# Moving the context's state and the first running sum to later levels inside the GLA heads of a hybrid backbone block

## Chip, cores and metric

The kernel runs on one core of one Trainium2 chip. The metric is the device time of one execution in microseconds (us). The engines are named as in the profile: PE is TensorE (matmul), PEld its weight loads, DVE VectorE, ACT ScalarE, POOL GpSimd, SP SyncE.

## What is computed

One backbone layer on 512 latent tokens and 256 context tokens of width 2048. One projection feeds four heads of gated linear attention (GLA, here *gated heads*) and four mLSTM heads, both run in two directions; an output projection, and a convolutional SwiGLU MLP follow. The gated heads, which the change concerns, compute this:

```python
def gla_scan(k, v, log_a, s0, q=None):      # chunked over CHUNK positions
    def step(s, inp):
        bcum = jnp.cumsum(ac, axis=2)
        b_end = bcum[:, :, -1, :]
        k_to_end = kc * jnp.exp(b_end[:, :, None, :] - bcum)
        s_new = jnp.exp(b_end)[..., None] * s + jnp.einsum('bhik,bhiv->bhkv', k_to_end, vc)
        ...
        scores = jnp.einsum('bhjk,bhik,bhjik->bhji', qc, kc, jnp.exp(rel))
        o = (jnp.einsum('bhji,bhiv->bhjv', scores, vc)
             + jnp.einsum('bhjk,bhkv->bhjv', qc * jnp.exp(bcum), s))
```

The context runs through this scan without queries; its last state is the state in which each latent scan begins. `log_a`, the decay, is a log-sigmoid of a low-rank projection.

## The kernel before

**Stages.** The program goes through modulation and the projections of heads 0 and 1 (to about 200 us), then a woven part (200 to 480 us), the mLSTM heads (to about 1060 us), the MLP (1076 to 2420 us) and a tail. The change lies in the woven part. There gated head *h* is worked on while PE also computes the projection of a later head: heads 0 and 1 beside the projection of head 2, head 2 beside that of head 3, head 3 and the gates of the mLSTM heads (`ml_gates`) beside that of head 4.

**Weaving.** `weave(stages, steps)` interleaves two generators. A stage yields how much PE time is wanted as cover, and `weave` takes steps of the projection until that debt is paid; what is overpaid stays as credit. A step is one *group* `a_0` to `a_5` of one pair of 128-row weight tiles (`kp`, 8 of them): a_0 and a_1 are six matmuls of 512 columns, a_2 and a_3 twelve of 256, a_4 and a_5 six of 384. They count as 1.36, 1.36, 1.44, 1.44, 1.04 and 1.04. The pair `fill` is what a gated head yields: `fill[0]` behind each level of scores, `fill[1]` behind each part between: (1.75, 0.85) in heads 0 and 1, (4.1, 2) in head 2, (2.7, 1.3) in head 3. In this part PE's instructions keep the program's order (`tc.keep_in_program_order`). The order on DVE, ACT and SP is chosen by a scheduler. All engines run their queue in order.

**One gated head** (`gla`). `sd` is the diagonal of the scores. Then seven levels of scores follow, 0 to 6: `ex` (decays; two DVE subtractions, two exponentials, a DVE product with q and k), matmuls `sl` (L801 to L804), and a DVE copy under a mask of `sl` into `sc` (L805). Between them stand:

- behind level 0, in head 0 only, `next(first, 1)` (L810): it makes the context's running sum `csum` on PE out of `cla`, and from it `kd`, the context's decay, by an exponential. `first` is `gla_prep(0)`, whose earlier steps made `cdec` (PE) and `cla` (DVE, L672). The other heads have all steps of `gla_prep` done by the head before: `after`, one step behind each of levels 2 to 6 (`dec` twice, PE, each with the `la` product on DVE L672; `cdec`, with `cla`; `csum`; the scans).
- behind level 1, the context's state `cst`: products of `kd` with the keys on DVE, eight matmuls on PE, a copy into `s0` on ACT (L818 to L825). Then `qi` and `kt` (decayed queries and keys for the latent states; ACT exponentials, DVE products).
- behind levels 2 and 3, `ktt`: a transposition of `kt` on PE and a copy on ACT (L846).
- behind levels 4 to 6, `st`: the latent states, matmuls on PE and two DVE products each (L856). The first of them reads `s0`.

At the end come the four outputs `po` (order 1, 2, 0, 3), for each a square on ACT (L869) and a copy to `ob` on DVE (L870), and later the transpositions `yt`.

**Banks.** The six groups of the projection hold six of the eight PSUM banks. All other PE results of the woven part (`sd`, `sl`, `dec`, `cdec`, `csum`, `cst`, `ktt`, `st`, `po`, `yt`, and `pre`, `pa`, `pgc` of `ml_gates`) share the other two through `psb`. So a matmul of these may start only when the reader of the bank's earlier owner is done.

**The splits.** Each `kp` needs its weights in two parts: `raw` arrives by DMA, ACT makes `hi_h` (L105), and DVE makes `lo_h` (L106), 1024 columns in one instruction.

**ml_gates** ends with two directions of the same: transpositions `pa` of `li` and `cum` (PE), `negh`, `negl` and `dg` (DVE, L928 to L932, from `pf`), and `pgc` (PE), which reads `dg`.

Of the kernel before, what the change touches and what calls it, by code (L numbers as in the profile page):

```python
# [18 lines left out]
P = 128  # L19
# [7 lines left out]
CJ = TC // P  # L27
H = 4
DK = 128
DV = 256  # L30
# [53 lines left out]
def block_kernel(ctx: ExitStack, tc: tile.TileContext, a: dict, out: bass.AP):  # L84
    nc = tc.nc
    V, S, G, PE = nc.vector, nc.scalar, nc.gpsimd, nc.tensor
# [9 lines left out]
    def mul(o, x, y):  # L96
        return V.tensor_tensor(out=o, in0=x, in1=y, op=ALU.mult).ins
# [12 lines left out]
    def mm(*args, **kw):  # L110
        ins = PE.matmul(*args, **kw)  # L111
        if pinned[0]:
            tc.keep_in_program_order(ins)

    def tr(*args):
        ins = PE.transpose(*args)
        if pinned[0]:
            tc.keep_in_program_order(ins)
# [8 lines left out]
    cst = keep.tile([P, C_END], F32, name="cst")  # L127
# [32 lines left out]
    def psb(name, shape=(P, T)):  # L160
        return banks8[0].tile(list(shape), F32, name=name, tag="acc") if banks8 else \
            psB.tile(list(shape), F32, name=name, tag="psb")

    def ytile(k, name, shape=(P, T), dtype=F32):
        return yp.tile(list(shape), dtype, name=name, tag=f"y{k}")
# [413 lines left out]
    first, early_sums = project_first()  # L579
# [40 lines left out]
    for c0, n, hs, m in ((0, T, hx, gm[0]), (T, TC, hc, gm[1])):  # L620
        ps = psb(f"gm{c0}", (P, n))
        for k in range(KT):
# [4 lines left out]
            for i, part in enumerate(parts):  # L627
                mm(ps[g : g + 32, :], wsm[:, k, :], part, start=(k < 4 and i == 0),
                   stop=(k >= 12 and i == len(parts) - 1), skip_group_check=True)
# [14 lines left out]
    def wtile(name, tag, *shape):  # L644
        return (wkh if tag in ("qk", "v", "kn", "vn") else wk).tile([P, *shape], F32, name=name, tag=tag)
# [110 lines left out]
    def level_decays(h, lv, bt):  # L756

        b = LEVELS[lv]
        n = T // (2 * b)
        ex = wk2.tile([P, 2, T], F32, name=f"ex{h}_{lv}", tag="ex")  # L760
        sf = bt[0].rearrange("p (n a b) -> p n a b", a=2, b=b)
        sb = bt[1].rearrange("p (n a b) -> p n a b", a=2, b=b)
        rf = sf[:, :, 0, b - 1 : b].unsqueeze(2).to_broadcast([P, n, 2, b])
        rb = sb[:, :, 1, 0:1].unsqueeze(2).to_broadcast([P, n, 2, b])
        sub(crossed(ex, b, True), sf[:, :, ::-1, :], rf)
        sub(crossed(ex, b, False), sb, rb)
        S.activation(ex[:, 0, :], ex[:, 0, :], AF.Exp, scale=DECAY)
        S.activation(ex[:, 1, :], ex[:, 1, :], AF.Exp, scale=-DECAY)
        return ex
# [5 lines left out]
    def gla(h, pair, qk, v, kn, vn, yT, prep, fill, after, pending, first=iter(())):  # L775
        bt, ends = prep["bt"], prep["ends"]

        sc = wtile(f"sc{h}", "sc", 2, TJ, P)
        scd = sc[:, 0]
        s0 = wtile(f"s0{h}", "state", 2, DV + 2)  # L780
        st = [s0[:, :, 0:DV], sc[:, 1].rearrange("p a b -> p (a b)").rearrange("p (d c) -> p d c", d=2)]
        mul(scd.rearrange("p a b -> p (a b)"), *qk)
        ps = psb(f"sd{h}", (P, TJ))
        for j in range(TJ):
            mm(ps[:, j : j + 1], scd[:, j, :], cst[:, C_ONE : C_ONE + 1], start=True, stop=True)
        V.scalar_tensor_tensor(out=scd, in0=ident.unsqueeze(1).to_broadcast([P, TJ, P]), scalar=2.0,
                               in1=ps.unsqueeze(2).to_broadcast([P, TJ, P]), op0=ALU.mult, op1=ALU.mult)
        yield fill[0]
        if next(first, 1) is None:
            yield fill[1]  # L790
        for lv, b in enumerate(LEVELS):
            ex = prep["ex"][lv] if lv < 2 else level_decays(h, lv, bt)
            if pair:
                done = mul(ex, ex, pair[0])
            else:
                for i in range(2):
                    done = mul(ex[:, i, :], ex[:, i, :], qk[i])
            if lv == 6:
                with tc.issue_after(done):
                    mul(qi, qi, qk[0].unsqueeze(1).to_broadcast([P, 2, T]))  # L800
            ps = psb(f"sl{h}_{lv}", (P, TJ, P))  # L801
            for i in range(TJ):
                js = slice(P * i, P * i + P)
                mm(ps[:, i, :], ex[:, 1, js], ex[:, 0, js], start=True, stop=True)  # L804
            done = V.copy_predicated(scd, msk[:, lv, :].unsqueeze(1).to_broadcast([P, TJ, P]), ps).ins  # L805
            if lv == 0:
                gate = done
            yield fill[0]
            if lv == 0:
                next(first, 1)  # L810
                for _ in pending:
                    pass
                yield fill[1]
            if lv > 1 and next(after, 1) is None:
                yield fill[1]
            if lv == 1:

                kd = prep["kd"]  # L818
                for j in range(CJ):
                    mul(kd[:, :, j], kd[:, :, j], kn[j].unsqueeze(1).to_broadcast([P, 2, DK]))  # L820
                ps = psb(f"cst{h}", (P, 2, DV))
                for d in range(2):
                    for j in range(CJ):
                        mm(ps[:, d, :], kd[:, d, j, :], vn[j][:, 0:DV], start=(j == 0), stop=(j == CJ - 1))
                S.copy(s0[:, :, 0:DV], ps)  # L825
                qi = wtile(f"qi{h}", "qi", 2, T)
                for d in range(2):
                    S.activation(qi[:, d, :], bt[d], AF.Exp, scale=DECAY)
                yield fill[1]
                kt = [ytile(10 + d, f"kt{h}{d}", (P, TJ - 1, P)) for d in range(2)]  # L830
                for d in range(2):
                    for i in range(TJ - 1):
                        S.activation(kt[d][:, i, :], bt[d][:, P * (i + d) : P * (i + d) + P], AF.Exp, scale=-DECAY,
                                     bias=ends[:, 0, d, i : i + 1])
                    x = kt[d].rearrange("p a b -> p (a b)")
                    with tc.issue_after(gate):
                        mul(x, x, qk[1][:, P * d : P * d + 3 * P])
                ktt = []
            elif lv in (2, 3):
                d = lv - 2  # L840
                ktt.append(ytile(12 + d, f"ktt{h}{d}", (P, TJ - 1, P)))
                ps = psb(f"ktt{h}{d}", (P, TJ - 1, P))
                for i in range(TJ - 1):
                    tr(ps[:, i, :], kt[d][:, i, :], ident)
                with tc.high_priority():
                    S.copy(ktt[d], ps)  # L846
                yield fill[1]
            elif lv > 3:
                n = lv - 4
                if n:  # L850
                    st.append(ytile(9 + n, f"st{h}{n}", (P, 2, DV)))
                ps = psb(f"st{h}{n}", (P, 2, DV))
                for d, i in ((0, n), (1, 2 - n)):
                    mm(ps[:, d, :], ktt[d][:, i, :], v[i + d][:, 0:DV], start=True, stop=True)
                for d, i in ((0, n), (1, 2 - n)):
                    V.scalar_tensor_tensor(out=st[n + 1][:, d, :], in0=st[n][:, d, :], scalar=ends[:, 1, d, i : i + 1],  # L856
                                           in1=ps[:, d, :], op0=ALU.mult, op1=ALU.add)
                yield fill[1]
        ssq = wtile(f"ssq{h}", "ssq", TJ)
        junk = wtile(f"junk{h}", "kn", DV)  # L860
        ob = wtile(f"ob{h}", "tmp", TJ, DV)
        for j in (1, 2, 0, 3):
            po = psb(f"po{h}_{j}", (P, DV))
            js = slice(P * j, P * j + P)
            parts = [(qi[:, d, js], st[3 - j if d else j][:, d, :]) for d in range(2)]
            parts.append((scd[:, j, :], v[j][:, 0:DV]))
            for n, (l, r) in enumerate(parts):
                mm(po, l, r, start=(n == 0), stop=(n == len(parts) - 1))
            S.activation(junk, po, AF.Square, accum_out=ssq[:, j : j + 1])  # L869
            V.tensor_copy(ob[:, j, :], po)  # L870
            yield 0.5
        return finish(h, ob, ssq, yT)
# [668 lines left out]
```

## Time and profile before

| | |
|---|---|
| time before, median of 3 runs | 2442.56 us (2441.49 to 2443.43) |
| the profiled execution's own time | 2441.44 us |
| its span in the trace | 2439.7 us |
| PE busy | 2412.9 us |
| DVE busy | 1793.3 us |
| ACT busy | 1005.2 us |
| mean granted clock of PE | 0.998 |

Times in the trace count from the start of the span. A row of the timeline has start, duration, engine, line, operation, what is written and read by the program's names without numbers, and in brackets the engine's idle time before it with what released it. Matmuls overlap: the next one starts before the modelled end of the last, so the time that a group of matmuls takes is read from its start to the next group's start. In the order of the program below, names carry numbers: `sl0_5` is the score of head 0 at level 5, `a2_1` is group 1 of the projection of head 2, `hi_h4_7` the weights of head 4 at kp 7.

### The profile page before, as it was taken

The numbers are of one execution on the slowest core, as the hardware profiler recorded it, in microseconds if no ns is written. First come the engines' busy times: TensorE is split into PE (matmuls) and PEld (weight loads), VectorE is DVE, ScalarE is ACT, GpSimd is POOL, SyncE is SP. The second block draws the span as 40 slices with busy tenths as digits, with TensorE's granted clock in tenths as the row PEclk, the third lists the DMA queues.
The fourth block names the chain that finished last, engine by engine and source line by source line (L and its number), as shares of the span: only waits on it lengthen the run. The fifth ranks groups of instructions, "written<-read, shape, count | busy, mean of one in ns | idle before, by whom it ended". The sixth has DMA issues, their size and how long they took to land.

```text
span 2439.7 us, 38673 instructions
## 1 busy us (share of the span) xinstructions
PE 2412.9 (99%) x15434; PEld 2173.7 (89%) x15434; DVE 1793.3 (74%) x2872; ACT 1005.2 (41%) x1498; POOL 175.9 (7%) x221
## 2 busy tenths in 40 slices
PE   8999999999999999999999999999999999999998
PEld 6888999899988888888898989899999999999997
DVE  6666856555456586779987887878787878787886
ACT  4225533322233232256544454445444444444445
POOL 0000000000000000000201010101011111111021
PEclk9999999999999999999999999999999999999999
DMA  9751111233455798833646464555555555546464
GB/s 388 284 173 56 46 53 44 78 121 114 137 189 191 237 321 275 287 130 109 145 132 154 116 151 123 137 134 141 136 130 139 134 143 122 146 123 154 113 185 135
DMA packets 122487, 373.67 MB, mean 153 GB/s; under 512 B 13912, under 2 KB 19010, under 8 KB 122306
## 3 DMA queue, kind: packets, MB, share of 16 engines
q1 hardware_dynamic: 95298, 318.75, 39.8%
q0 software_dynamic: 25920, 51.40, 11.7%
q8 instruction: 121, 1.98, 0.3%
q10 hardware_dynamic: 1088, 1.05, 0.1%
q14 instruction: 60, 0.49, 0.1%
HBM read 320.80 MB, written 50.34 MB: 152 GB/s over the span
## 4 chain that ended last, share of the span: by engine, by line
PE 94%; DVE 3%; DMA 1%; ACT 1%; issue 1%; SPq 0%; POOL 0%; POOLq 0%; ACTq 0%; DVEq 0%
PE a L111 19%; PE ug L111 18%; PE uv L111 18%; PE dn L111 18%; PE ga L111 7%; PE wo L111 7%; PE po L111 2%; PE ps_m L111 1%; PE sl L111 1%; PE st L111 1%; PE cst L111 1%; DMA raw_uv<-in_w_up 0%; DVE ex L94 0%; DMA xl<-in_xT 0%; DMA raw_m<-in_w_mod 0%
## 5 line engine op out<-in xcount | busy, mean ns | idle before, releaser
L111 PE MATMUL dn<-gh,lo_d 128*128 128x512 f32 x672 | 262.5, 391 | 2.3 <-DVE lo_d L106 2.3
L111 PE MATMUL dn<-gl,hi_d 128*128 128x512 f32 x672 | 261.6, 389 | 0.0
L111 PE MATMUL dn<-gh,hi_d 128*128 128x512 f32 x672 | 261.6, 389 | 0.0
L1295 DVE SCALAR_TENSOR_TENSOR cv<-pads,cwt,cv 128x512 f32<-128x512 f32 x344 | 239.2, 747 | 0.6
L1349 POOL DMA_DIRECT2D x2d<-st x160 | 140.1, 929 | 1142.0 <-ACT st L1348 1062.2
L106 DVE TENSOR_TENSOR lo_buv<-sum_uv,hi_buv 128x1024 fp32r<-128x1024 f32 x80 | 98.0, 1225 | 102.8 <-ACT hi_buv L105 102.7
L322 DVE SCALAR_TENSOR_TENSOR raw_m<-raw_m,crow 128x1024 f32<-128x1024 f32 x128 | 154.6, 1229 | 1.7 <-DMA raw_m<-in_w_mod 1.7
L111 PEld LDWEIGHTS dn<-gh,lo_d 128*128 128x128 f32 x672 | 126.1, 188 | 31.1 <-DVE lo_d L106 5.2
L111 PE MATMUL a<-hi_h,hTh 128*128 128x256 f32 x512 | 151.7, 296 | 0.5 <-ACT e L404 0.5
L111 PEld LDWEIGHTS dn<-gl,hi_d 128*128 128x128 f32 x672 | 126.2, 188 | 26.0
L111 PEld LDWEIGHTS dn<-gh,hi_d 128*128 128x128 f32 x672 | 126.2, 188 | 25.7
L111 PE MATMUL a<-lo_h,hTh 128*128 128x256 f32 x512 | 144.7, 283 | 0.0
L111 PE MATMUL a<-hi_h,hTl 128*128 128x256 f32 x512 | 144.6, 283 | 0.0
L105 ACT CAST hi_d<-raw_d 128x1024 fp32r<-128x1024 f32 x86 | 88.6, 1030 | 130.0 <-PE ug L111 70.3
L106 DVE TENSOR_TENSOR lo_d<-raw_d,hi_d 128x1024 fp32r<-128x1024 f32 x86 | 102.9, 1196 | 48.3 <-ACT hi_d L105 47.8
L111 PE MATMUL ug<-bth,hi_bug 128*128 128x256 f32 x480 | 136.8, 285 | 0.0
L111 PE MATMUL ug<-bqh,lo_aug 128*128 128x256 f32 x480 | 135.8, 283 | 0.0
L111 PE MATMUL uv<-bqh,lo_auv 128*128 128x256 f32 x480 | 135.8, 283 | 0.0
L111 PE MATMUL uv<-bth,hi_buv 128*128 128x256 f32 x480 | 135.8, 283 | 0.0
L111 PE MATMUL uv<-btl,hi_buv 128*128 128x256 f32 x480 | 135.8, 283 | 0.0
L111 PE MATMUL uv<-bth,lo_buv 128*128 128x256 f32 x480 | 135.8, 283 | 0.0
L111 PE MATMUL uv<-bql,hi_auv 128*128 128x256 f32 x480 | 135.8, 283 | 0.0
(414 smaller groups left out, 7262.7 us busy)
## 6 DMA issues: line engine op xcount, KB each, us to landing
raw_m<-in_w_mod SPq DMA_DIRECT2D x192, 512.0 KB, 5.1
raw_d<-in_w_down SPq DMA_DIRECT2D x82, 512.0 KB, 3.5
raw_ug<-in_w_up SPq DMA_DIRECT2D x80, 512.0 KB, 3.6
x2d<-st POOLq DMA_DIRECT2D x160, 256.0 KB, 5.6
raw_uv<-in_w_up SPq DMA_DIRECT2D x80, 512.0 KB, 5.4
raw_h<-in_w_heads SPq DMA_DIRECT2D x64, 512.0 KB, 3.6
raw_ga<-in_w_gates SPq DMA_DIRECT2D x32, 512.0 KB, 3.8
raw_wo<-in_w_out SPq DMA_DIRECT2D x32, 512.0 KB, 4.5
```

The lines of the kernel that those rows point to most:

```text
L105: cast[0] = S.copy(hi, x).ins
L106: return V.tensor_tensor(out=lo, in0=x, in1=hi.bitcast(F32), op=ALU.subtract).ins
L111: ins = PE.matmul(*args, **kw)
L322: V.scalar_tensor_tensor(out=x, in0=x, scalar=1.0, in1=crow[0], op0=ALU.mult, op1=ALU.mult, accum_out=mtot[:, at : at + 1])
L1295: V.scalar_tensor_tensor(out=t3, in0=src, scalar=w, in1=t3, op0=ALU.mult, op1=ALU.add)
L1349: nc.gpsimd.dma_start(x2d[k], t, accum_op=ALU.add)
```

## The change

Three things are altered in `gla`. The running sum of the first head is made behind level 1 instead of level 0. The context's state is made behind level 2 instead of level 1, in all four gated heads. And one more `yield fill[1]` stands behind it (in the old place one followed `qi`, and that one stays), so that each head asks for one more cover.

```diff
             if lv == 0:
-                next(first, 1)
                 for _ in pending:
                     pass
                 yield fill[1]
             if lv > 1 and next(after, 1) is None:
                 yield fill[1]
             if lv == 1:
-
-                kd = prep["kd"]
-                for j in range(CJ):
-                    mul(kd[:, :, j], kd[:, :, j], kn[j].unsqueeze(1).to_broadcast([P, 2, DK]))
-                ps = psb(f"cst{h}", (P, 2, DV))
-                for d in range(2):
-                    for j in range(CJ):
-                        mm(ps[:, d, :], kd[:, d, j, :], vn[j][:, 0:DV], start=(j == 0), stop=(j == CJ - 1))
-                S.copy(s0[:, :, 0:DV], ps)
+                next(first, 1)
                 qi = wtile(f"qi{h}", "qi", 2, T)
...
             elif lv in (2, 3):
+                if lv == 2:
+                    kd = prep["kd"]
+                    for j in range(CJ):
+                        mul(kd[:, :, j], kd[:, :, j], kn[j].unsqueeze(1).to_broadcast([P, 2, DK]))
+                    ps = psb(f"cst{h}", (P, 2, DV))
+                    for d in range(2):
+                        for j in range(CJ):
+                            mm(ps[:, d, :], kd[:, d, j, :], vn[j][:, 0:DV], start=(j == 0), stop=(j == CJ - 1))
+                    S.copy(s0[:, :, 0:DV], ps)
+                    yield fill[1]
                 d = lv - 2
```

Every engine issues the same instructions as before, PE 14663 matmuls and DVE 2746 instructions among them; only the order differs, from level 1 of head 0 to the end of `ml_gates`. POOL's order is the same. On SP one load (of `wlr3`) moves ahead of two weight loads of head 3. The old and the new order differ in many rows; three places follow.

The first is PE's order in head 0 at level 1, as a piece of the difference (`-` before, `+` after); `csum0` is the running sum, and the a2 rows belong to the projection of head 2.

```order
 L111 MATMUL a2_2_2070<-lo_h2_1_2178,hTh3_579 128x256
 L111 MATMUL a2_2_2070<-hi_h2_1_2177,hTl3_580 128x256
-L111 MATMUL csum0_2219<-cla0_2076,cst_58 128x128 x6
-L111 MATMUL sl0_1_2229<-ex0_1_2155 128x128 x4
+L111 MATMUL sl0_1_2220<-ex0_1_2155 128x128 x4
 L111 MATMUL a2_3_2071<-hi_h2_1_2177,hTh2_569 128x256
 L111 MATMUL a2_3_2071<-lo_h2_1_2178,hTh2_569 128x256
```

`csum0` no longer stands between the group a_2 and `sl0_1`; it comes after a_3 and a_4, where `cst0` stood, and `cst0` comes just ahead of the transposition `ktt00`.

The second is PE's order around level 5 of head 0, in two pieces of the difference: `cdec1` belongs to the preparation of head 1, `st00` to the states of head 0.

```order
 L111 MATMUL a2_0_2068<-hTl7_965,hi_h2_3_2405 128x512
 L111 MATMUL a2_0_2068<-hTh7_964,lo_h2_3_2406 128x512
-L111 MATMUL cdec1_2415<-wlr1_2306,glr_92 128x256 x2
-L111 MATMUL st00_2422<-v0_2057,ktt00_2325 128x256
-L111 MATMUL st00_2422<-v0_2057,ktt01_2373 128x256
+L111 MATMUL cdec1_2415<-wlr1_2298,glr_92 128x256 x2
 L111 MATMUL a2_1_2069<-hTh6_954,hi_h2_3_2405 128x512
 L111 MATMUL a2_1_2069<-hTl6_955,hi_h2_3_2405 128x512
```

Before, `cdec1` and `st00` stood together ahead of the group a_1; after, `cdec1` alone. The end of that group follows:

```order
 L111 MATMUL a2_1_2069<-hTl7_965,hi_h2_3_2405 128x512
 L111 MATMUL a2_1_2069<-hTh7_964,lo_h2_3_2406 128x512
+L111 MATMUL st00_2428<-v0_2057,ktt00_2325 128x256
+L111 MATMUL st00_2428<-v0_2057,ktt01_2379 128x256
 L111 MATMUL sl0_5_2439<-ex0_5_2433 128x128 x4
 L111 MATMUL a2_2_2070<-hi_h2_3_2405,hTh6_954 128x256
```

`st00` now stands right ahead of the scores `sl0_5`. In the compiled programs `sl0_5` used the bank of `st00` before and uses that of `cdec1` after; at level 5 of head 1 it is the same with `cdec2`.

The third place is the end of `ml_gates`. On PE, around `pa0` and `pgc0` in the first direction, before:

```order
 L111 MATMUL a4_1_3732<-hTl15_1785,hi_h4_7_4365 128x512
 L111 MATMUL a4_1_3732<-hTh15_1784,lo_h4_7_4366 128x512
-L116 MATMUL pa0_4382<-cst_58,li_4202 128x4 x6
-L116 MATMUL pa0_4382<-cst_58,cum_4205 128x4 x4
 L111 MATMUL a4_2_3733<-hi_h4_7_4365,hTh14_1774 128x256
 L111 MATMUL a4_2_3733<-lo_h4_7_4366,hTh14_1774 128x256
```

and at the end of the twelve matmuls of that group a_2:

```order
 L111 MATMUL a4_2_3733<-lo_h4_7_4366,hTh15_1784 128x256
 L111 MATMUL a4_2_3733<-hi_h4_7_4365,hTl15_1785 128x256
-L111 MATMUL pgc0_4413<-dg_4381,cst_58 128x16
+L116 MATMUL pa0_4394<-cst_58,li_4208 128x4 x6
+L116 MATMUL pa0_4394<-cst_58,cum_4211 128x4 x4
+L111 MATMUL pgc0_4413<-dg_4393,cst_58 128x16
 L111 MATMUL a4_3_3734<-hi_h4_7_4365,hTh14_1774 128x256
 L111 MATMUL a4_3_3734<-lo_h4_7_4366,hTh14_1774 128x256
```

Before, the group a_2 stood between `pa0` and `pgc0`; after, they are neighbours. On DVE at the same place, before:

```order
L911 SCALAR_TENSOR_TENSOR pf_4203<-li_4202 4x768 x2
L928 TENSOR_SCALAR negh_98<-pf_4203 4x512
L100 TENSOR_TENSOR cum_4205<-cum_4205,pf_4203 36x768
L929 SCALAR_TENSOR_TENSOR negl_99<-pf_4203,negh_98 4x512
L932 TENSOR_SCALAR dg_4381<-cst_58,pf_4203 4x4 x4
L928 TENSOR_SCALAR negh_98<-pf_4203 4x512
L106 TENSOR_TENSOR lo_h5_0_4492<-raw_h5_0_4489,hi_h5_0_4491 128x1024
```

and after (line numbers are higher by one behind the change):

```order
L912 SCALAR_TENSOR_TENSOR pf_4209<-li_4208 4x768 x2
L929 TENSOR_SCALAR negh_98<-pf_4209 4x512
L100 TENSOR_TENSOR cum_4211<-cum_4211,pf_4209 36x768
L106 TENSOR_TENSOR lo_h5_0_4492<-raw_h5_0_4489,hi_h5_0_4491 128x1024
L930 SCALAR_TENSOR_TENSOR negl_99<-pf_4209,negh_98 4x512
L933 TENSOR_SCALAR dg_4393<-cst_58,pf_4209 4x4 x4
L929 TENSOR_SCALAR negh_98<-pf_4209 4x512
```

The split `lo_h5_0` (for the projection of head 5) stood behind `dg` and now stands between the sum `cum` and `negl`, ahead of `dg`.

## Prediction

> **What bounds the kernel.** On the page I read first the chain of waits that ended last, as shares of the span.
>
> ```profile
> PE 94%; DVE 3%; DMA 1%; ACT 1%; issue 1%; SPq 0%; POOL 0%; POOLq 0%; ACTq 0%; DVEq 0%
> ```
>
> PE is the bound, and the change removes no PE work: it can only take away or add times in which PE stands still. So the second view is what PE waited for between 180 and 480 us (us in total, times, longest), and the third the windows of 20 us from 180 to 500, whose sum line is quoted.
>
> ```profile
> PE csum L111 <- DVE cla L672: 0.9, 1, 0.9
> PE sl L111 <- ACT ktt L846: 0.7, 1, 0.7
> PE po L111 <- DVE st L856: 0.6, 1, 0.6
> PE pa L116 <- DVE cum L100: 0.5, 1, 0.5
> PE sl L111 <- DVE sc L856: 0.4, 1, 0.4
> PE po L111 <- DVE ob L870: 0.4, 1, 0.4
> sum 320.00, PE 316.55 PEld 286.21 DVE 217.32 ACT 135.11 POOL 4.03; mean PE 19.78 PEld 17.89 DVE 13.58 ACT 8.44 POOL 0.25
> ```
>
> In these 320 us PE is idle for 320.00 − 316.55 = 3.45 us. The six stops make 3.5 of it. This is the most that the change could win in idle time, and it is 0.14% of 2442.56; 0.2% (4.9 us) is about what a measurement of this kernel can tell from no change. What the change adds has no such limit. So I followed PE's new order through the woven part, with times of the old one: at each place where the order differs, when does PE arrive, and when is what it needs ready? Times below are differences to the old run at the same work.
>
> **Head 0, level 1.** The timeline of PE and of DVE around the running sum:
>
> ```profile
> 215.44 0.72 DVE L805 COPY_PREDICATED sc<-msk,sl 128x512 f32<-128x512 uint8 x1
> 216.06 0.68 DVE L672 SCALAR_TENSOR_TENSOR cla<-cdec,ct 128x512 f32<-128x512 f32 x1
> 216.88 1.58 PE L111 MATMUL csum<-cla,cst 128*128 128x128 f32 x12 [0.88 <-DVE cla L672]
> 218.29 1.06 PE L111 MATMUL sl<-ex 128*128 128x128 f32 x8
> 219.10 0.36 PE L111 MATMUL a<-hi_h,hTh 128*128 128x256 f32 x1
> 220.62 0.34 PE L111 MATMUL a<-hi_h,hch 128*128 128x384 f32 x1
> ```
>
> `csum` waits until 216.88 for `cla`, 0.88 us. Steps from start to start: `csum` 218.29 − 216.88 = 1.41, `sl` 0.81, a group a_3 1.52. After the change `sl` of level 1 comes first. It needs the bank of level 0's `sl`, free when the mask copy ends: 215.44 + 0.72 = 216.16. PE is there at 216.88 − 0.88 = 216.00, so it waits some 0.2 us. `csum` comes after that `sl` and two groups and waits for nothing. That is −0.7. The second stop, 0.66 us behind `ktt` (`sl <- ktt`), goes too: the old `sl` of level 3 stood directly behind `ktt`, the new one has a group a_2 between. But level 2's `sl` now meets its `ex` product about as late as PE arrives; I give 0.4 back. Sum for levels 1 to 4: −1.0, bounds −1.5 (both stops, nothing back) and 0.
>
> **Head 0, level 5.** Now `sl` takes the bank of `cdec`, whose reader is `cla`:
>
> ```profile
> 238.32 0.40 PE L111 MATMUL cdec<-wlr,glr 98*128 98x256 f32 x2
> 240.88 0.69 DVE L672 SCALAR_TENSOR_TENSOR cla<-cdec,ct 128x512 f32<-128x512 f32 x1
> 240.98 0.35 PE L111 MATMUL sl<-ex 128*128 128x128 f32 x1
> ```
>
> Before, `sl` started 240.98 − 238.32 = 2.66 behind `cdec`, and `cla` ended 240.88 + 0.69 − 238.32 = 3.25 behind it. Nobody waited, as `sl` had another bank. With this bank PE waits 0.6 at the least; DVE has its two `st` products to do as well, and a_1 and `st` end later, so I take 0.95. The range is 0 (DVE does `cla` at once) to 1.5. That uses up what level 1 gave.
>
> **The outputs of head 0, the start of head 1.**
>
> ```profile
> 255.67 0.70 PE L111 MATMUL po<-st,qi 128*128 128x256 f32 x2 [0.57 <-DVE st L856]
> 259.91 0.69 DVE L97 TENSOR_TENSOR sc<-e,e 128x512 f32<-128x512 f32 x1 [0.36 <-PE po L111]
> ```
>
> `po` number 2 waited 0.57 for `st`. It now comes a group later relative to `st`'s product, so this goes, with the slow group ahead of it −0.9. But `sd` of head 1 now follows the last `po` with no group between, and its input `sc` is made by DVE only when `po` has ended (the second row: released by `po`, 0.69 long). PE waits 0.36 + 0.69 and the passing on, some 1.2, where the group a_2 hid it. Of these I count +1.0. Net +0.1, bounds −0.9 and +0.7.
>
> **Head 1.** Two new waits and one gain.
>
> ```profile
> 221.67 1.89 PE L111 MATMUL cst<-vn,kd 128*128 128x256 f32 x8
> 223.21 0.53 PE L111 MATMUL a<-hi_h,hch 128*128 128x384 f32 x1
> 275.04 0.40 PE L111 MATMUL dec<-glr,wlr 98*128 98x512 f32 x1
> 275.28 0.28 PE L111 MATMUL a<-hi_h,hTh 128*128 128x256 f32 x1
> 277.90 0.68 DVE L672 SCALAR_TENSOR_TENSOR la<-dec,lt 128x512 f32<-128x512 f32 x1
> 285.93 0.40 PE L111 MATMUL cdec<-wlr,glr 98*128 98x256 f32 x2
> 289.03 0.38 PE L111 MATMUL sl<-ex 128*128 128x128 f32 x1 [0.41 <-DVE sc L856]
> 289.50 0.68 DVE L672 SCALAR_TENSOR_TENSOR cla<-cdec,ct 128x512 f32<-128x512 f32 x1
> 303.00 0.59 PE L111 MATMUL po<-st,qi 128*128 128x256 f32 x2
> 306.15 0.48 PE L111 MATMUL po<-st,qi 128*128 128x256 f32 x1 [0.40 <-DVE ob L870]
> 307.37 0.53 PE L111 MATMUL a<-hi_h,hch 128*128 128x384 f32 x1
> ```
>
> At level 2 the order is now `dec`, a_4, `cst`, `ktt`. With two banks, `ktt` takes that of `dec`, whose reader `la` ends 277.90 + 0.68 − 275.04 = 3.54 behind `dec`. PE is there after `dec` (275.28 − 275.04 = 0.24), a_4 (221.67 − 220.62 = 1.05) and `cst` (223.21 − 221.67 = 1.54), 2.83: it waits 0.7, of which I take 0.6 (0 to 0.9). At level 5 `sl` again takes the bank of `cdec`: `cla` ended 289.50 + 0.68 − 285.93 = 4.25 behind it, `sl` itself started 3.10 behind (with a stop of 0.41). With the bank's wait that is 1.15 to 1.45 more, less if DVE's new order brings `cla` forward (0). I take 1.1. The gain is at the outputs: the last `po` took 307.37 − 306.15 = 1.22, but the two before it 306.15 − 303.00 = 3.15, 0.7 more than twice that, and the last waited 0.40 for a copy to `ob`. A group a_5 now stands between the second and the third: −1.0 (−1.3 to −0.5). Head 1: +0.7.
>
> **Heads 2 and 3.** All six stops lie outside them, since a larger `fill` puts more groups between. Head 2 loses the group between its outputs 2 and 0; four `po` in a row then wait for copies to `ob` as head 1's did. I take half of head 1's 1.0, +0.5 (0 to 1.0). Head 3: +0.1. On SP the small load of `wlr3` passes two weight loads of head 3; no stop in the waits above is one for a transfer, so this costs nothing as long as the splits, which hide it, run ahead of PE. The products with `kd` on DVE and the copy into `s0` on ACT move along with `cst`; the reader of `s0`, `st`'s product behind level 4, is still two levels away, and PE's matmuls between cover it.
>
> **The gates** hold the largest term. The wait for `pa`'s input and what follows, on PE and on DVE:
>
> ```profile
> 468.65 0.94 DVE L100 TENSOR_TENSOR cum<-cum,pf 36x768 f32<-36x768 f32 x1
> 469.52 0.67 DVE L929 SCALAR_TENSOR_TENSOR negl<-pf,negh 4x512 fp32r<-4x512 f32 x1
> 470.12 0.60 DVE L932 TENSOR_SCALAR dg<-cst,pf 4x4 f32<-4x4 f32 x4
> 471.20 1.23 DVE L106 TENSOR_TENSOR lo_h<-raw_h,hi_h 128x1024 fp32r<-128x1024 f32 x1
> 469.64 0.41 PE L116 MATMUL pa<-cst,cum 4*128 4x4 f32 x4 [0.45 <-DVE cum L100]
> 469.98 0.39 PE L111 MATMUL a<-hi_h,hTh 128*128 128x256 f32 x1
> 471.60 0.39 PE L111 MATMUL pgc<-dg,cst 4*128 4x16 f32 x2
> ```
>
> The sum `cum` starts at 468.65 and releases `pa` 0.99 later. `pa` takes 469.98 − 469.64 = 0.34, a_2 takes 1.62, and `pgc` found `dg` long done (470.72). As many groups stand between the gates' inputs `pre` and `pa` as before, so `pa` meets `cum` as before. But `pgc` now follows `pa` directly, 0.99 + 0.34 = 1.33 behind the start of `cum`, and on DVE the split of head 5 has come between: `cum` 0.87 (to the next start), the split 1.2, `negl` 0.60, `dg` 0.60, together 3.27. PE stands 3.27 − 1.33 = 1.94 before `pgc`. a_2 is not gone but moved ahead of `pa`. +2.0; without the split it would be 1.94 − 1.2 = 0.7, the lower end; the upper is 2.4, the wait of 0.45 for `cum` once more.
>
> [...]
>
> **Sum.** −1.0 + 0.95 + 0.1 + 0.7 + 0.5 + 0.1 + 2.0 = +3.35, of which I keep 3.2, as the first two places share a stop. From 480 us on the order is the same and PE is full, so nothing gives it back. The profiled execution took 2441.44 us (1.7 around its span), 1.12 below the median; a profiled run of the new kernel would take 2444.6, and the median 2442.56 + 3.2 = 2445.8. By the single bounds the sum runs from −2.5 to +7; all at one end is unlikely, so I take +1.0 to +5.2 for this case alone, of which the part over 4.9 is small.
>
> **Rivals.**
>
> *The clock closes (slower).* PE's granted clock falls when its work grows thin, as the start of the run shows (columns: window; length, busy PE, PEld, DVE, ACT, POOL; clock, DMA share, GB/s):
>
> ```profile
> 16.00:24.00 8.00, 5.16 (x56) 1.97 (x54) 5.78 (x10) 1.69 (x3) 0.00 (x0) 1.00 1.03 417
> 24.00:30.00 6.00, 4.55 (x33) 3.59 (x34) 3.18 (x9) 3.14 (x5) 0.00 (x0) 0.77 1.03 407
> 240.00:260.00 20.00, 19.43 (x116) 17.09 (x115) 18.57 (x33) 9.05 (x23) 0.00 (x0) 1.00 0.19 58
> ```
>
> After 8 us with 5.16 busy the clock was 0.77 for 6 us: 6 × 0.23 = 1.4 us lost. If the stop before `pgc` and the ones in head 1 have the same effect, two such events add 2.8: 3.2 + 2.8 = +6.0, 2448.5. It decides from stops together of some 2.8 us in 8 us, 8 − 5.16, which is more than I count in any 8 us; so 0.12. [...]
>
> *DVE falls behind and stays behind (slower).* DVE was busy 217.32 of 320 us, so it catches up in the mean; but where `cla` and `la` hold a bank, each later `sl` could wait as well. Each of the two waits in head 1 would then come twice (+1.7), and the outputs gain nothing (+1.0): +5.9, 2448.5. It decides where the mask copy behind each `sl` runs late by more than the group between. 0.12.
>
> *The change removes stops and adds none.* The five stops in heads 0 and 1: 0.88 + 0.66 + 0.57 + 0.41 + 0.40 = 2.9, which gives 2439.7. For this DVE would have to serve `cla`, `la` and `dg` ahead of the splits; the rows show the splits in front. 0.08; of it 0.03 for slow groups beside the stops vanishing as well, beyond −4.9.
>
> *Only the gates' stop fails to come,* since the split lands elsewhere in time: 3.2 − 2.0 = +1.2, 2443.8. 0.1.
>
> **Chances.** The forecast has 0.58, of which 0.07 lies over 4.9. Slower by over 0.2%: 0.07 + 0.12 + 0.12 = 0.31, less 0.02 for the second and third case falling short: 0.29. Faster: 0.03. Within 0.2%: 0.68. The predicted time is 2445.8. The range leaves out the case of no new stops and the upper end of the slow ones, from +0.4 to +6.4: 2443.0 to 2449.0. The likeliest case's own range is 2443.6 to 2447.8.
>
> **What would show it.** In the profile of the new kernel: no `csum <- cla` in the waits; `sl` of level 5 of heads 0 and 1 behind `cla`, 0.6 to 1.4 us each; `ktt` of head 1 behind `la`; `sd` of head 1 behind `sc`, about 1 us; `pgc <- dg` with about 1.9 us, the longest; PE idle of 6 to 7 us between 180 and 500 instead of 3.45. The prediction is wrong if that idle time stays under 4, if the clock of a 20 us window there falls under 0.98, or if the time changes outside 200 to 480 us.

## The result and the profile after

The changed kernel takes 2449.24 us, median of 7 runs (2448.8 to 2450.83), beside 2441.55 of the kernel before in the same series (2440.27 to 2443.43): ratio 1.0031, 95% interval 1.0022 to 1.0040. It is slower by 7.7 us. The forecast was 2445.8 with a range to 2449.0, and "within 0.2%" as the likeliest outcome. The profiled execution of the changed kernel has a span of 2447.3 us, 7.6 longer than before. The two profiles count the same instructions on both sides, 15434 matmul records on PE and 2872 on DVE (not the 14663 and 2746 named above).

The waits of PE between 180 and 490 us in the changed kernel (us in total, times, longest):

```profile
PE sl L111 <- DVE cla L672: 2.4, 2, 1.8
PE pgc L111 <- DVE dg L933: 2.0, 1, 2.0
PE sd L111 <- DVE sc L97: 0.8, 1, 0.8
PE ktt L116 <- DVE la L672: 0.6, 1, 0.6
PE pa L116 <- DVE cum L100: 0.5, 1, 0.5
PE sl L111 <- DVE ex L97: 0.4, 1, 0.4
PE sl L111 <- DVE sc L805: 0.3, 1, 0.3
PE po L111 <- DVE ob L871: 0.2, 1, 0.2
```

`csum <- cla` is gone, as it should be, and so are `sl <- ktt`, `po <- st` and the wait of `sl` for `sc` of L856. Six new waits stand in their place (`pa` is as before), all of them foreseen by name. Where the time is lost can be read from starts of the same instruction in the two traces. `sd` opens heads 1, 2 and 3, and by then both orders have done the same work; `pg` stands behind the gates. First the kernel before, then the changed one (timeline of PE):

```profile
261.14 0.95 PE L111 MATMUL sd<-cst,sc 128*128 128x1 f32 x8
312.42 0.72 PE L111 MATMUL sd<-cst,sc 128*128 128x1 f32 x6
394.41 0.83 PE L111 MATMUL sd<-cst,sc 128*128 128x1 f32 x7
482.71 0.50 PE L111 MATMUL pg<-negh,pick 4*128 4x512 f32 x2
```

```profile
261.36 0.83 PE L111 MATMUL sd<-cst,sc 128*128 128x1 f32 x6 [0.79 <-DVE sc L97]
314.12 0.95 PE L111 MATMUL sd<-cst,sc 128*128 128x1 f32 x8
396.54 0.61 PE L111 MATMUL sd<-cst,sc 128*128 128x1 f32 x5
475.61 0.36 PE L111 MATMUL pgc<-dg,cst 4*128 4x16 f32 x2 [1.95 <-DVE dg L933]
475.90 0.38 PE L111 MATMUL a<-hi_h,hTh 128*128 128x256 f32 x1
489.57 0.50 PE L111 MATMUL pg<-negh,pick 4*128 4x512 f32 x2
```

The lag, by which the changed kernel starts the same instruction later, is 0.22 us at head 1, 1.70 at head 2, 2.13 at head 3, and 475.61 − 471.60 = 4.01 at `pgc`. Up to here it is the waits. But at `pg`, 14 us later, it is 6.86, and no row of the waits accounts for those 2.85 us. The windows do. They are cut here so that their edges fall on the changes of the clock (length, busy PE, PEld, DVE, ACT, POOL; granted clock; DMA share; GB/s):

```profile
470.26:473.67 3.41, 2.90 (x25) 2.50 (x23) 3.38 (x4) 0.60 (x1) 0.00 (x0) 1.00 0.00 0
473.67:477.08 3.41, 1.47 (x12) 1.48 (x13) 3.35 (x10) 0.27 (x2) 0.00 (x0) 1.00 0.47 141
477.08:480.49 3.41, 3.41 (x20) 3.17 (x19) 1.17 (x8) 0.85 (x3) 0.00 (x0) 0.50 0.03 13
480.49:483.90 3.41, 3.41 (x12) 2.94 (x11) 0.58 (x2) 0.97 (x2) 0.00 (x0) 0.50 0.00 0
483.90:487.31 3.41, 3.41 (x18) 2.91 (x19) 3.37 (x11) 0.67 (x3) 0.00 (x0) 1.00 0.22 44
```

After a stretch with 1.47 of 3.41 us busy, PE ran at half clock for twice 3.41 us (6.83 in the trace's record of the clock). PE counts as fully busy there, so this loss is in no list of waits: only the column of the clock shows it.

The last 0.7 us lie outside the woven part. The same clock halves once more at the norm ahead of the MLP, where PE has matmuls of one column (0.50 from 1081.24 to 1084.65 us); in this execution of the kernel before it did not (1.00 from 1064.90 to 1084.00). `ps_rms` opens the norm, `ug` the MLP:

```profile
1070.02 0.47 PE L111 MATMUL ps_rms<-cst,sqsq 128*128 128x1 f32 x3 [0.21 <-DVE sqsq L100]
1076.76 0.50 PE L111 MATMUL ug<-bqh,hi_ug 128*128 128x512 f32 x1
```

```profile
1076.91 0.24 PE L111 MATMUL ps_rms<-cst,sqsq 128*128 128x1 f32 x1 [0.21 <-DVE sqsq L100]
1085.02 0.70 PE L111 MATMUL ug<-bqh,hi_ug 128*128 128x512 f32 x2
```

The lag goes from 6.89 to 8.26, and the MLP gives 0.7 of it back. The code is the same on both sides of the change here. In the profiled executions of the kernels below, whose code there is the same too, all six with a fall at the gates showed this one as well, and of the five without one three did (the change in heads 0 to 2, one added instruction, the last version) and two did not. Whether these 0.7 us belong to the change is therefore not shown; the work of PE ahead of this fall is taken up at the end.

### The profile page after: what moved, and what is told of

Its sections match the earlier page's. It is cut to its first block, busy times and chain, and to the rows that moved or that the text cites. A ratio compares the mean times of both kernels' runs of the same rounds, so it can differ in the third digit from the quotient of the medians.

```text
span 2447.3 us, 38669 instructions
## 1 busy us (share of the span) xinstructions
PE 2417.3 (99%) x15434; PEld 2177.2 (89%) x15434; DVE 1792.9 (73%) x2872; ACT 1006.0 (41%) x1498; POOL 176.0 (7%) x221
## 4 chain that ended last, share of the span: by engine, by line
PE 86%; issue 6%; DVE 4%; DMA 2%; ACT 1%; POOL 0%; SPq 0%; POOLq 0%; ACTq 0%; DVEq 0%
PE a L111 18%; PE uv L111 16%; PE dn L111 15%; PE ug L111 15%; PE ga L111 7%; PE wo L111 7%; PE po L111 2%; DVE cv L1296 1%; PE ps_m L111 1%; PE sl L111 1%; PE st L111 1%; DMA raw_m<-in_w_mod 1%; DVE lo_d L106 1%; DMA raw_uv<-in_w_up 1%; PE cst L111 0%
```

## Experiments

All medians below are of 8 to 11 runs; the kernel before ran beside them and had 2441.71, 2441.52 and 2441.62 us in the three series.

**Which heads lose what.** First the change in head 3 alone (the conditions `h == 3` at the three edits), as a difference to the changed kernel, with lines left out at the dots.

```diff
             if lv == 0:
+                if not (h == 3):
+                    next(first, 1)
...
+            if lv == 1 and not (h == 3):
+                kd = prep["kd"]
...
             if lv == 1:
-                next(first, 1)
+                if h == 3:
+                    next(first, 1)
...
-                if lv == 2:
+                if lv == 2 and (h == 3):
```

> The change in head 3 alone (heads 0 to 2 as before). The loss is taken to have three parts: 2.1 us from new waits in heads 0 to 2, 1.9 us from the stop before pgc, 2.9 us because PE's clock closes behind that stop (plus 0.7 us outside the woven part). Theory: the last two hang on head 3's extra cover alone, which puts the group a_2 ahead of pa; so here no new waits before 440 us, pgc waits about 2 us for dg, the granted clock falls near 0.5 for some 6 us behind it, and the time is 4 to 6 us above before. Rival: the clock closes because of all the stops together, those of heads 0 to 2 included; then only the stop of 1.9 us comes, the clock stays at 1.00, and the time is about 2 us above before.

2446.50 us, ratio 1.0018 (1.0009 to 1.0027), 4.8 above. Its profile has the waits of the kernel before and one more, and one window of half clock behind it:

```profile
PE pgc L111 <- DVE dg L945: 2.0, 1, 2.0
```

```profile
470.13:473.54 3.41, 0.96 (x11) 0.80 (x10) 3.38 (x9) 0.27 (x2) 0.00 (x0) 0.99 0.31 38
473.54:476.95 3.41, 3.41 (x19) 3.17 (x18) 2.34 (x11) 0.42 (x1) 0.00 (x0) 0.50 0.30 115
476.95:480.36 3.41, 3.41 (x23) 3.07 (x23) 0.71 (x4) 1.34 (x5) 0.00 (x0) 1.00 0.01 2
```

The theory holds: without any new stop in heads 0 to 2 the clock falls. Here it stayed down for one window of 3.41 us, not for the 6 us expected; the runs spread from 2443.18 to 2448.26, wider than those of the changed kernel.

The other part, the change in heads 0 to 2 alone (`h < 3` in the same places):

> The change in heads 0 to 2 alone (head 3 as before). Theory: new waits of heads 0 to 2, 2.1 us in all (0.2 by the start of head 1, 1.7 by the start of head 2, 2.1 by the start of head 3), then nothing more: pgc waits for nothing, the clock stays at 1.00, and the time is 1.5 to 3 us above before. Rival: what is late in the heads makes DVE late in the gates, and the stop and the clock come here too: 5 to 8 us above.

2443.88 us, ratio 1.0009 (1.0001 to 1.0018), 2.2 above. `pgc` waits for nothing and the clock is 1.00 throughout the gates. The two parts add up: 4.8 + 2.2 = 7.0, against 7.7 for the whole change.

**Which of the edits costs.** The moves without the added cover:

```diff
                     S.copy(s0[:, :, 0:DV], ps)
-                    yield fill[1]
```

> The moves of the running sum and of the context's state without the added cover (yield). Theory: the cover, which shifts every later group by one place, costs the time, and the moves themselves cost nothing; the stop of csum (0.9) goes, a wait of some 0.3 us of ktt for la comes in head 1, gates and clock are as before: 0 to 1 us below before. Rival: the moved work costs (cst right ahead of ktt, in banks that are not free): the waits of head 1 come here too, 1.5 to 2 us above before.

2441.02 us, ratio 0.9998 (0.9989 to 1.0007): no change. The waits show why a move that takes away the longest stop wins nothing. What `csum` no longer waits for, waits of `sl` in heads 0 and 1 take back, 1.0 of them for the state's product (0.4 before):

```profile
PE sl L111 <- DVE sc L856: 1.0, 2, 0.6
PE sl L111 <- DVE ex L97: 0.6, 2, 0.4
PE sl L111 <- ACT s L839: 0.3, 1, 0.3
```

All waits of PE there make 3.1 us, where the kernel before has 3.5, and the lag at the gates is −0.1: nothing that the runs can tell. And the cover alone, with both pieces of work left where they were:

```diff
             elif lv in (2, 3):
+                if lv == 2:
+                    yield fill[1]
                 d = lv - 2
```

> The added cover alone (a yield behind level 2), with the running sum and the context's state where they were before. Theory: nearly the whole loss: sl of level 5 in heads 0 and 1 waits for cla, pgc waits 2 us for dg, the clock falls near 0.5 behind it; 6 to 8 us above before. Rival (the moves cost the time): at most 1 us above before.

2447.84 us, ratio 1.0026 (1.0016 to 1.0037), 6.2 above. So four fifths of the loss come from a line that adds no instruction: it shifts every later group by one place against the heads' own work. Its profile has `sl <- cla` with 2.8, `pgc <- dg` with 2.0, and three windows of half clock (473.45 to 483.68).

**Is it the bank?** The changed kernel, with one ACT copy that takes the result of `dec` and `cdec` out of its bank at once; the order on PE is the same.

```diff
     def log_sigmoid(o, ps, t):
+        if ps is not o:
+            S.copy(o, ps)
+            ps = o
         S.activation(t, ps, AF.Abs)
```

> The changed kernel with one added ACT copy for each dec and cdec: their result leaves its PSUM bank at once, and the log-sigmoid reads it from SBUF. The order on PE is the same. Theory (sl of level 5 and ktt wait only because cla and la hold the bank): the waits of sl for cla (2.4 us) and of ktt for la (0.6) go, 2.5 to 3 us less before head 2; the stop at pgc and the clock stay: 3.5 to 5.5 us above before. Rival (PE meets a DVE that is late as a whole, and the bank is only the first thing it waits for): the waits come back under other names, and less than 1 us is won.

2448.35 us, ratio 1.0025 (1.0016 to 1.0033), 6.8 above: less than 1 us won, as the rival said. Yet the waits it was made to remove are gone, and another has come:

```profile
PE sl L111 <- DVE ex L97: 3.4, 2, 1.8
PE pgc L111 <- DVE dg L936: 2.0, 1, 2.0
```

Between level 2 and level 6 of head 1 this kernel loses nothing, where the changed kernel loses 2.2 us: `sl` of level 5 starts there at 291.57, before `cla` (293.74), so it was the bank and not `cla` itself. But the added copies put ACT's exponentials of head 0 back (those of level 0 begin at 212.57 us, in the changed kernel at 210.72), and at levels 0 and 2 PE waits 3.4 us for `ex`, 3.0 more than in the changed kernel. Both theories were half right: the bank was the cause of the waits, and freeing it through a second engine was no cure. The trace of the changed kernel shows the chain that holds the bank in head 1:

```profile
288.34 0.40 PE L111 MATMUL cdec<-wlr,glr 98*128 98x256 f32 x2
290.13 1.22 DVE L716 TENSOR_TENSOR_SCAN bt<-cst,la 128x512 f32<-128x512 f32 x1
291.26 0.45 DVE L857 SCALAR_TENSOR_TENSOR sc<-s,ends,st 128x256 f32<-128x256 f32 x1
291.64 0.68 DVE L672 SCALAR_TENSOR_TENSOR cla<-cdec,ct 128x512 f32<-128x512 f32 x1
292.47 0.80 PE L111 MATMUL sl<-ex 128*128 128x128 f32 x5 [1.80 <-DVE cla L672]
```

**What the stop at pgc is, and what cures it.** The changed kernel with less cover ahead of `pa` (`yield 10.2` for `yield 11.4`), so that a_2 stands between `pa` and `pgc` again:

> The changed kernel with one number altered: the cover ahead of the transpositions pa is 10.2 instead of 11.4, so that the group a_2 stands between pa and pgc again; DVE's order keeps the split ahead of dg. Theory: pgc's stop shrinks from 1.95 to about 0.3 us and with it the clock stays open: the 2.1 us of heads 0 to 2 remain, 2 to 4 us above before. Rival (DVE's split ahead of dg is what costs, wherever a_2 stands): the stop stays near 2 us and the time within 1 us of the changed kernel's.

2447.20 us, ratio 1.0018 (1.0009 to 1.0027), 5.7 above. Neither theory: `pgc` waits no more, but `pa` does.

```profile
PE pa L116 <- DVE cum L100: 1.9, 1, 1.9
```

The stop moved one place ahead, with the same length, and the clock fell behind it as well (for 3.4 us). PE comes to the end of DVE's chain too early; a group that is taken from ahead of `pa` is missing there. So the opposite was tried, a group more between `pa` and `pgc` and nothing taken away:

```diff
-            yield 1.4
+            yield 2.0 if d == 0 else 1.4
             pg = psb(f"pgc{d}", (P, TJ, H))
```

> The changed kernel with one number altered: the cover between pa and pgc of the first direction is 2.0 instead of 1.4, so that the group a_3 stands between them. Nothing else moves on PE up to there, and DVE's order keeps the split ahead of dg. Theory (the loss behind the heads is the bare stop at pgc, and the clock's fall is due to it): the stop shrinks from 1.95 to about 0.4 us, the clock stays at 1.00, and only the 2.1 us of heads 0 to 2 remain with it: 2 to 3.5 us above before, like the change in heads 0 to 2 alone. Rival (the clock falls because of the long thin stretch of pa, and the cover comes too late): the clock falls all the same, 5 to 7 us above.

2444.03 us, ratio 1.0012 (1.0003 to 1.0021), 2.4 above: what heads 0 to 2 cost, and no more. The wait is down to a sixth, and the granted clock is 1.00:

```profile
PE pgc L111 <- DVE dg L933: 0.3, 1, 0.3
```

```profile
474.40:477.80 3.40, 3.07 (x23) 2.62 (x21) 3.35 (x10) 0.69 (x3) 0.00 (x0) 1.00 0.43 152
```

One number of cover wins back 5.3 of the 7.7 us, of which the stop itself is 1.6.

**When the clock falls.** To measure the clock by itself, the kernel before was given one, two and three needless DVE instructions in the chain that makes `dg` (the first as shown, the others repeat it on `ab`), and nothing else.

```diff
+            g0 = gmx
+            if d == 0:
+                g0 = ab
+                V.tensor_tensor(out=ab, in0=gmx, in1=gmx, op=ALU.max)
...
-                V.tensor_scalar(out=dg[rows[d], n, :], in0=e, scalar1=gmx[rows[d], end : end + 1], scalar2=None,
+                V.tensor_scalar(out=dg[rows[d], n, :], in0=e, scalar1=g0[rows[d], end : end + 1], scalar2=None,
```

> The kernel before with one added DVE instruction in the chain of dg (ab, 0.95 us), so that pgc waits about 1.3 us. With two of them the stop was 2.64 us and the clock fell to half for about 6 us; with none there is no stop. Theory now (the clock falls when a stop fills most of a window of some 3 us whose phase is not fixed): 1.3 us are too little, the clock stays at 1.00, the time is 1 to 2 us above before. Rival (stops add up with pa's 0.45 and the small matmuls): half clock for some 3 us here too, 2.5 to 4.5 us above.

> The kernel before, with two added DVE instructions (ab, 36x768, about 0.95 us each; their result has the value that dg reads anyway) in the chain that makes dg. The order on PE is that of before: a_2 stands between pa and pgc. dg should end some 5.5 us behind the start of cum, so pgc waits about 2.5 us with a full group of matmuls right ahead. Theory (the clock closes only when some 3.3 us pass with nearly no work in the array, and the small transpositions pa count as none): the stop lasts 2.5 to 2.9 us with pgc, so the clock stays at 1.00 and the time is 2 to 3 us above before. Rival (stops add up, whatever stands between them): here 0.45 + 2.5 us within 6 us are more than the 2.45 us of the changed kernel, so the clock falls near 0.5 for 3 to 7 us and the time is 4 to 6 us above.

> As the kernel before with three such added DVE instructions, so that pgc waits about 4 us behind a full group. Both theories of the clock expect it to fall here: 4 us of stop, and 1.6 to 3.3 us for the half clock behind it, 5.5 to 7.5 us above before. If the clock stays at 1.00 (4 us above), a pure stop does not close it and the small matmuls of pa and pgc are part of the cause.

With one: a stop of 1.2 us, 2443.11 us, ratio 1.0008 (0.9999 to 1.0017), 1.5 above, the clock in the gates at 1.00. With two: 2.6 us, 2447.03 us, ratio 1.0020 (1.0011 to 1.0030), 5.5 above. With three: 4.2 us, 2449.98 us, ratio 1.0030 (1.0020 to 1.0040), 8.5 above. The stops, in the same order:

```profile
PE pgc L111 <- DVE dg L938: 1.2, 1, 1.2
```

```profile
PE pgc L111 <- DVE dg L938: 2.6, 1, 2.6
```

```profile
PE pgc L111 <- DVE dg L938: 4.2, 1, 4.2
```

The window ahead of the fall, with two instructions, and of those behind it the first and the first at full clock:

```profile
471.85:475.26 3.41, 1.21 (x9) 1.22 (x10) 3.28 (x10) 0.00 (x0) 0.00 (x0) 1.00 0.48 154
475.26:478.67 3.41, 3.41 (x20) 3.17 (x19) 1.10 (x9) 0.85 (x3) 0.00 (x0) 0.50 0.00 0
...
482.08:485.49 3.41, 3.41 (x18) 2.90 (x18) 1.86 (x4) 1.22 (x2) 0.00 (x0) 1.00 0.01 2
```

A stop of 1.2 us cost about itself (1.5), as far as the runs can tell it from nothing. Stops of 2.6 and 4.2 us cost 5.5 and 8.5, themselves and some 3 to 4 us more, with the clock at 0.50 behind them. The expectation of the theory for two instructions was wrong: a full group of matmuls right ahead of the stop did not save the clock, and no 3.3 us with nearly no work (in the changed kernel 475.61 − 472.28 = 3.33, from the end of the last group's matmul to `pgc`) were needed: the stop was of 2.6 us. Nor is the length of a stop all that counts. The changed kernel's stop of 1.80 us in head 1 left PE hardly busier than the window ahead of its fall, and the clock stayed at 1.00, in the traces of all five kernels that have this stop:

```profile
289.35:292.76 3.41, 1.61 (x9) 1.18 (x8) 3.41 (x7) 2.52 (x6) 0.00 (x0) 1.00 0.00 0
```

**A version with all of this.** The moves without the heads' cover, and in the gates a group more both ahead of `pa` (12.8) and ahead of `pgc` (2.8):

> The two moves without the added cover in the heads, and in the gates one group more ahead of pa (12.8 instead of 11.4) and one between pa and pgc (2.8 instead of 1.4). Theory: the stops of csum (0.9) and of pa (0.45) go and pgc waits for nothing: 0.3 to 1 us below before, less than the runs can tell apart. Rival: the later pgc delays what reads it in head 4, and the time is 1 us or more above before.

2441.28 us, ratio 0.9998 (0.9989 to 1.0006). `pa` waits no more, and the last lag is 0.1 us or less. No version was found that is faster than the kernel before by anything the runs can tell.

## Why the prediction was wrong

Its direction was right, but 3.2 us were forecast and 7.7 measured. Its method, following PE's new order with the old times, came close on nearly every wait. Term by term, with the lag read from the starts of the same instruction, less the groups that one order has done ahead of the other:

| term | forecast | measured |
|---|---|---|
| head 0, levels 1 to 4 | −1.0 | −0.9 |
| head 0, level 5 | +0.95 | +0.8 |
| outputs of head 0, `sd` of head 1 | +0.1 | +0.2 |
| head 1 | +0.7 | +1.5 |
| head 2, head 3 | +0.6 | +0.4 |
| the stop at `pgc` | +2.0 | +1.9 |
| sum of the waits (0.1 of lag was there at the start) | +3.35 | +3.9 |
| half clock behind the gates | 0 | +2.85 |

- *Head 1* was too small by 0.8. `ktt` behind `la` cost 1.0 with the slower `cst` ahead of it (0.6 forecast), `sl` of level 5 cost 1.4 (1.1 forecast), and the outputs gave back 0.65 (1.0). For the second I had allowed the early end of the range; DVE put a scan and a product ahead of `cla` instead.
- *The gates* came out as worked: the split stood in the chain, and `pgc` waited 1.95 us, forecast 1.94.
- *The step that failed* is the clock, which the sum put at nothing and which took 2.85 us behind the gates. That a stop of 1.94 us costs no more than its own length there was the author's estimate, and no run shows it: behind the stop of 1.95 us the clock was 0.50 for 6.83 us. The rival "The clock closes" named the place, and its time, 2448.5, is 0.7 from the measured one; but that is partly luck. It priced two falls of 1.4 us, one at the gates and one at head 1. There was one, of two windows, at the gates, and none at head 1. It was given only 0.12, because it was to decide "from stops together of some 2.8 us in 8 us". The runs show a lower point: 2.45 us of stops at `pa` and `pgc`, and 1.9 us alone in the kernel with less cover, closed it; 1.2 us there, and 1.8 us in head 1, did not. The two rows from the start of the run were read too coarsely. The clock there fell at 27.25 for 3.41 us, which costs up to 1.7 us (the 1.4 counts only the part up to 30.00), and in the 3.41 us right ahead of it, behind the row with 5.16 of 8, PE was busy for 1.80 us. So 1.61 us of idle time were enough there, less than the forecast stop of 1.94:

```profile
23.84:27.25 3.41, 1.80 (x21) 0.84 (x21) 0.79 (x3) 0.82 (x2) 0.00 (x0) 1.00 1.02 414
27.25:30.66 3.41, 3.41 (x15) 3.28 (x15) 3.21 (x7) 2.98 (x5) 0.00 (x0) 0.50 1.06 401
```

- *The signs named beforehand.* PE was idle for 320.00 − 312.66 = 7.3 us between 180 and 500, where 6 to 7 were expected. The sign of being wrong came: the clock was 0.93 and 0.90 in the two windows of 20 us from 460 on.
- *The windows.* In every fall at the gates the clock was 0.50 for 3.41 us or a multiple of it. None of the windows of 3.41 us ahead of these falls was idle: PE was busy 0.96 to 2.23 us in them.
- *The other rivals.* DVE did not stay behind: the lag stands at 1.70 through all of head 2 up to its outputs. No case without new waits came. That the split might land elsewhere did not happen.
- *The limit on gains* held: the moves alone, without the cover, won nothing that the runs can tell.
- *The bounds.* The single bounds add up to −2.9 and +7.55, not −2.5 and +7; the range that was taken does not rest on this.

What stays open: which work holds the clock up. PE's busy time alone does not tell. A window with 2.23 of 3.41 us busy (the cover alone) came ahead of a fall, and the one of head 1 with 1.61 did not. What the windows ahead of a fall share is said in the last section; no kernel was made to test it.

## What to carry to other kernels

A stop of PE can have a price beyond its length. In the gates 1.2 us cost itself here, and stops from 1.9 us on cost 1.4 to 4.3 us more (5.7 less 2.4 and 1.9 with less cover; 8.5 less 4.2 with three instructions); in head 1, with no small matmuls beside it, 1.8 us cost only itself. So a forecast for the gates of this kernel needs a second term for a stop of 1.9 us; between 1.2 and 1.9 us no run was made. The column of the granted clock must be read beside the waits, since PE counts as busy for 3.41 of 3.41 us at a clock of 0.50. In this woven order, a line that only asks for more cover is not free (6.2 us): it moves every later piece by one group, and so decides which wait meets cover and which stands bare; put cover where the chain of another engine ends, and try it one place at a time.

## What was not expected of the hardware

The half clock came in whole windows. In seven kernels whose clock fell at the gates it stayed at 0.50 for 3.4 us (the change in head 3; less cover ahead of `pa`), 6.8 us (the changed kernel; two added instructions) or 10.2 us (the cover alone; the copies out of the bank; three added instructions), never for anything between. How many windows it takes is not set by the stop alone: the same stop of 1.95 us gave one, two and three of them.

The windows lay on one grid through a run, as far as its falls and rises can be timed: they are whole multiples of 3.413 us apart. In the changed kernel it was 453.97 us at full clock between the fall at the start and that at the gates (133 windows), and 597.33 between the gates and the norm (175). The falls at the gates and at the norm lie 604.16 us apart with the change in head 3 alone (177) and 607.6 with the cover alone (178). Where the grid lay against the program differed between two executions: the clock first fell at 27.25 us in the kernel before and at 19.69 in the changed one, whose order is the same up to level 1 of head 0; that is 2.2 windows apart. On this grid the falls sorted by the time that PE is busy with *wide* matmuls, those of more than 16 columns, that is, without `pa`, `pgc`, `sd` and the norm's `ps_rms`. From 40 to 2400 us, the windows ahead of the 17 falls, at the gates and at the norm, had 0.00 to 1.57 of 3.41 us of wide matmuls, all but one at most 1.41 us; the lowest window without a fall had 1.49 in the kernel before (the norm, at 1068.32) and 1.61 in the changed one (the stop of head 1, at 289.35). The length of the falls sorted the same way: a window at half clock was followed by another where this time was at most 2.33 us (9 windows) and by full clock where it was 2.92 or more (17). So what a thin stretch cost in these traces went with how the grid cut it, at the gates as at the norm. The limit of 16 columns was chosen with the traces in hand, so this is a sorting of these executions and not a test.
